# One piece each for the state and the output products of an S5 quarter, at high priority

## The chip, the cores and the metric

The kernel runs on one core of a Trainium2 chip. The metric is the device time of one execution in microseconds (us), as the median of several runs. One execution is also profiled; its trace has start and length of every instruction on TensorE (PE; PEld is its weight load), VectorE (DVE), ScalarE (ACT), GpSimd (POOL) and SyncE (SP), and of the DMA issues.

## The reference, cut to what matters

A decoder trunk of two layers over 256 positions of width 2048. Layer 0 joins dilated softmax attention and gated linear attention. Layer 1, in which the change lies, joins S5 state-space groups with HGRN2 gated linear recurrence:

```
def cd_layer(h, ...):
    z = h @ w_in
    u, qd, fd, idd, gate = jnp.split(z, CD_SPLIT, axis=-1)
    yc = s5_mixer(u, ...)
    f = lower_bound + (1.0 - lower_bound) * jax.nn.sigmoid(fd)
    od = chunked_gated_linear_attention(silu(qd), 1.0 - f, idd, jnp.log(f))
    yd = head_rmsnorm(od, hgrn_norm_g)
    y = jnp.concatenate([yc, yd], axis=-1) * jax.nn.silu(gate)
    return y @ w_out

def s5_mixer(u, ...):      # 64 groups of 16 channels, 64 complex states each
    bu = einsum(bb, u)                     # state products
    x = associative_scan(a * x + bu)       # complex, over positions
    y = c_re x_re - c_im x_im + d_skip * u # output products
    y = gelu(y)
    return y * sigmoid(y @ w_glu + b_glu)
```

## The kernel before

**Weights.** Almost all time is matrix products with streamed weights. `gemm_fm` (L181) and `gemm_tm` (L200) take a weight block in groups of four K-tiles of 128. `load_split` loads a group (`raw`, on SP, three buffers) and cuts it into two *pieces* of two K-tiles. For each piece ScalarE rounds `raw` to `wh` (L168) and VectorE makes the rest `wl = raw - wh` (L169), both urgent and with three buffers. A piece is 24 products of 128x256 in `gemm_fm` or 12 of 128x512 in `gemm_tm`; the first third of them need no `wl`. So ScalarE and VectorE can be at most three pieces ahead, and a `wh` or `wl` can be written only when TensorE has used up the piece three before.

**Hooks.** At the end of each piece `hook()` takes the next *slot* of the list `fillq` and issues what stands in it behind the last product (`issue_after`). The slots hold the S5 work.

**S5.** The 64 groups are done in four quarters, first to fourth, each with eleven slots. In a quarter (`s5_quarter`) `load0` loads the table W (tile `tb`) and the input X; the state products `v_mm` (L583) go to PSUM; VectorE multiplies them with rotation tables (L589 to L592), adds (L601, L602), scans (L603, L604), turns back (L605 to L608), writes X for the outputs (L611) and the sum t2 (L612). The output products `y_mm` are L622 (from X) and L627 (from t2). `finish` copies them to `ys` (ScalarE, L635), writes them to DRAM `s5y` in eight small DMAs (L638; POOL and ScalarE's queue, which also runs ScalarE's work), reads them back in another layout as `yc` (L641, POOL) and forms the GELU: `gw` on ScalarE (L643, L644, L646, L647), L645 and L649 on VectorE. Tables and `yc` have one buffer each. PSUM tiles for all this (`pm`) are four.

**HGRN2.** Beside it, in program order between the weight products, run the two halves of the gated linear attention (`gla`): evacuation of q and k (L359), activations on ScalarE (L666 to L672), `gQ` (L279) and `gT` (L327), then levels h = 1, 2, 4, ..., each with small products on TensorE (L287, L308, L316), a predicated copy (L296) and two multiplications that the next level needs (L324, L325), then L339.

**Order.** The kernel is written in one order; a scheduler that simulates the engines sets the order of each engine's queue by priority and by what it takes to be ready. On the chip each engine works strictly in that order. `urgent()` lifts the priority to the highest. Work without it goes by its place in the program.

## Time and profile before

| | |
|---|---|
| median of 3 runs | 894.18 us (888.37, 894.18, 894.41) |
| profiled execution | 894.61 us, of which the span of the trace 892.7 us |
| granted TensorE clock, mean | 0.996 |
| busy share of the span | PE 98%, DVE 71%, ACT 53%, POOL 6% |
| S5 quarters' products | from 509.9 us to 660.5 us of the span |

The busy share of TensorE is time in which a product runs, small ones too. A row of the timeline has start, length, engine, line, tiles and count, and in brackets the idle time before it with what ended it. The trace counts each product on f32 data of the S5 part as two passes (32 passes for 16 instructions); the rounded weight products take one.

### The profile page before, as it was taken

The numbers are of one execution on the slowest core, as the hardware profiler recorded it, in microseconds if no ns is written. First come the engines' busy times: TensorE is split into PE (matmuls) and PEld (weight loads), VectorE is DVE, ScalarE is ACT, GpSimd is POOL, SyncE is SP. The second block draws the span as 40 slices with busy tenths as digits, with TensorE's granted clock in tenths as the row PEclk, the third lists the DMA queues.
The fourth block names the chain that finished last, engine by engine and source line by source line (L and its number), as shares of the span: only waits on it lengthen the run. The fifth ranks groups of instructions, "written<-read, shape, count | busy, mean of one in ns | idle before, by whom it ended". The sixth has DMA issues, their size and how long they took to land.

```text
span 892.7 us, 18688 instructions
## 1 busy us (share of the span) xinstructions
PE 874.1 (98%) x7728; PEld 804.5 (90%) x7728; DVE 636.0 (71%) x1197; ACT 473.1 (53%) x715; POOL 54.4 (6%) x106
## 2 busy tenths in 40 slices
PE   8999999999999999999999999999999999999995
PEld 8987899888998899999999999899867899988894
DVE  7987975888869868755575586877977655665562
ACT  7654546665655765644443345455545475444451
POOL 0001100111101101000000001100110000000000
PEclk9999999999999999999999999999999999999998
DMA  9827744777756655555575766754654455544432
GB/s 316 318 99 217 257 159 146 231 253 217 264 193 220 223 179 182 206 189 189 190 270 195 267 211 227 247 192 166 222 170 160 183 189 189 189 171 179 176 136 94
DMA packets 40388, 180.40 MB, mean 202 GB/s; under 512 B 12720, under 2 KB 14256, under 8 KB 22768
## 3 DMA queue, kind: packets, MB, share of 16 engines
q1 hardware_dynamic: 29440, 154.99, 49.5%
q0 software_dynamic: 7984, 22.69, 7.7%
q10 hardware_dynamic: 2880, 1.54, 0.6%
q8 instruction: 60, 0.98, 0.4%
q14 instruction: 24, 0.20, 0.1%
HBM read 166.48 MB, written 12.71 MB: 201 GB/s over the span
## 4 chain that ended last, share of the span: by engine, by line
PE 74%; DVE 8%; ACT 6%; DMA 5%; issue 5%; SPq 0%; POOL 0%; POOLq 0%; DVEq 0%; ACTq 0%
PE pg L181 48%; PE pg L200 17%; DVE wl L169 2%; PE pg L758 2%; DMA tabs<-pc 2%; ACT wh L168 1%; PE pm L287 1%; DMA E<-ed 1%; PE pm L339 1%; DMA s5y<-ys 1%; ACT bb L1021 1%; DMA raw<-in_w_dram 1%; ACT x L1039 1%; PE pm L308 1%; DVE PP L1005 1%
## 5 line engine op out<-in xcount | busy, mean ns | idle before, releaser
L168 ACT ACTIVATE wh<-raw 128x1024 fp32r<-128x1024 f32 (+2 forms) x276 | 287.6, 1046 | 325.0 <-PE pg L181 187.6
L169 DVE TENSOR_TENSOR wl<-raw,wh 128x1024 fp32r<-128x1024 f32 (+2 forms) x276 | 332.6, 1207 | 173.7 <-ACT wh L168 165.0
L181 PE MATMUL pg<-xh,wh 128*128 128x256 f32 x1024 | 162.8, 281 | 1.8 <-ACT wh L168 1.7
L181 PE MATMUL pg<-xl,wh 128*128 128x256 f32 x1024 | 163.8, 280 | 0.0
L181 PE MATMUL pg<-xh,wl 128*128 128x256 f32 x1024 | 163.4, 281 | 0.1
L181 PEld LDWEIGHTS pg<-xh,wh 128*128 128x128 f32 x1024 | 137.4, 188 | 3.7 <-ACT wh L168 3.1
L181 PEld LDWEIGHTS pg<-xl,wh 128*128 128x128 f32 x1024 | 138.0, 188 | 0.8 <-issue 0.3
L181 PEld LDWEIGHTS pg<-xh,wl 128*128 128x128 f32 x1024 | 137.9, 189 | 0.8 <-DVE wl L169 0.3
L200 PE MATMUL pg<-wh,xh 128*128 128x512 f32 x320 | 100.4, 395 | 1.8 <-ACT wh L168 1.8
L200 PE MATMUL pg<-wl,xh 128*128 128x512 f32 x320 | 101.0, 396 | 0.5 <-DVE wl L169 0.4
L200 PE MATMUL pg<-wh,xl 128*128 128x512 f32 x320 | 101.0, 395 | 0.0
L200 PEld LDWEIGHTS pg<-wh,xh 128*128 128x128 f32 x320 | 59.3, 188 | 14.8 <-ACT wh L168 2.2
L200 PEld LDWEIGHTS pg<-wl,xh 128*128 128x128 f32 x320 | 59.5, 188 | 14.1 <-DVE wl L169 1.3
L200 PEld LDWEIGHTS pg<-wh,xl 128*128 128x128 f32 x320 | 59.9, 188 | 12.8
L181 PE MATMUL pg<-yh,wh 128*128 128x256 f32 x320 | 50.8, 281 | 0.0
L181 PE MATMUL pg<-yl,wh 128*128 128x256 f32 x320 | 50.6, 281 | 0.0
L181 PE MATMUL pg<-yh,wl 128*128 128x256 f32 x320 | 50.6, 281 | 0.0
L181 PEld LDWEIGHTS pg<-yl,wh 128*128 128x128 f32 x320 | 43.4, 190 | 0.1
L181 PEld LDWEIGHTS pg<-yh,wh 128*128 128x128 f32 x320 | 43.2, 189 | 0.1
L181 PEld LDWEIGHTS pg<-yh,wl 128*128 128x128 f32 x320 | 43.1, 189 | 0.0
L967 POOL DMA_DIRECT2D tabs<-pc x44 | 23.8, 546 | 167.0 <-DVE x L977 43.7
L200 PE MATMUL pg<-wh,yh 128*128 128x512 f32 x96 | 30.1, 394 | 0.0
(350 smaller groups left out, 994.0 us busy)
## 6 DMA issues: line engine op xcount, KB each, us to landing
raw<-in_w_dram SPq DMA_DIRECT2D x100, 1024.0 KB, 5.0
raw<-in_wo_dram SPq DMA_DIRECT2D x28, 1024.0 KB, 4.8
tb<-tabs POOLq DMA_DIRECT2D x8, 768.0 KB, 6.4
tabs<-pc POOLq DMA_DIRECT2D x20, 256.0 KB, 5.7
raw<-in_wg_dram SPq DMA_DIRECT2D x4, 1024.0 KB, 4.8
raw<-in_wo1l_dram SPq DMA_DIRECT2D x4, 1024.0 KB, 4.8
raw<-in_w_dram SPq DMA_DIRECT2D x6, 512.0 KB, 7.4
tabs<-pc POOLq DMA_DIRECT2D x24, 128.0 KB, 4.9
```

The source lines that it names most:

```text
L168: state["wh"] = A.activation(w, r, AF.Copy)
L169: V.tensor_sub(l, r, w)
L181: state["mm"] = T.matmul(ps[:, c], w[:, cs], a[:, kt], start=(i == 0 and n == 0 and c % 2 == 0), stop=(i == last and n == 2), skip_group_c ...
L200: state["mm"] = T.matmul(ps[:, t], a[:, kt, ts_], w, start=(i == 0 and n == 0), stop=(i == last and n == 2), skip_group_check=True)
L287: T.matmul(ps[32 * b:32 * b + 32, t, hd], k[:, hd, r], Q[:, hd, r], start=True, stop=True)
L308: T.matmul(ps[j0:j0 + h, hd, j0 + h:j0 + 2 * h], k[:, hd, b:b + h], Qp[:, hd, b + h:b + 2 * h], start=True, stop=True)
L339: T.matmul(ps[:, (hd - h0) * dv:(hd - h0 + 1) * dv], AT[:, hd, t + j], v[:, j, hd * dv:(hd + 1) * dv], start=(j == 0), stop=(j == t))
L758: T.matmul(ps[:, t, 0:256], a_[:, kt, ts_], w_, start=(kt == 0 and n == 0), stop=(kt == KT - 1 and n == 2), skip_group_check=True)
L967: nc.gpsimd.dma_start(tabs[qt, dst, n], t[src].rearrange("p a b -> p (a b)"))
L1005: V.scalar_tensor_tensor(PP[half[1 - g], g].rearrange("p a b c -> p (a b c)"), x1[half[g]], -1.0, x2[half[g]], op0=OP.mult, op1=OP.subtract)
L1021: A.activation(bb[half[g ^ n], g], z[n][half[g]].unsqueeze(2).to_broadcast([64, 8, 4, 16]), AF.Copy)
L1039: A.activation(v8(x1)[:, r_], cst[:, C_ID64:C_ID64 + 64], AF.Copy, scale=vec[:, V_D + 8 * qt + r_:V_D + 8 * qt + r_ + 1])
```

## The change

Before, a quarter's state products stood in two slots (each in two calls), the second with half of the products' evacuation, and its output products in two more. Now `v_mm` holds all 32 state products in one call, under `urgent()`, with two PSUM tiles at once, and the eight multiplications behind them; it stands in the first slot together with the scan. `y_mm` holds all output products, first all of L622 and then all of L627 (L620 and L625 after), under `urgent()`, in the slot of what was the second half.

```
-        def v_mm(h, n):
-            def go():
-                if n == 0:
-                    t["pv"] = pm_tile()...
-                for w in range(2):
-                    for pr in range(2 * n, 2 * n + 2):
-                        ...T.matmul(pv[...], t["W"][w][us, 4 * h + pr], X[us, g, 4 * h + pr], ...)
-                if n == 1:
-                    V.tensor_mul(t1[:, hs], pv[:, 0], Rc[:, hs])
...
+        def v_mm():
+            X = t["X"]
+            pvs = [pm_tile().rearrange("p (w r c) -> p w r c", w=2, r=4) for _ in range(2)]
+            with urgent():
+                for h, pv in enumerate(pvs):
+                    for w in range(2):
+                        for pr in range(4):
+                            for g in range(2):
+                                us = slice(64 - g * 64, 128 - g * 64)
+                                T.matmul(pv[g * 64:g * 64 + 64, w, pr], t["W"][w][us, 4 * h + pr],
+                                         X[us, g, 4 * h + pr], start=True, stop=True)
+            for h, pv in enumerate(pvs):
+                V.tensor_mul(t1[:, hs], pv[:, 0], Rc[:, hs])
...
-        def y_mm(n):
...
-                for pr in range(4 * n, 4 * n + 4):
+        def y_mm():
+            t["py"] = py = pm_tile().rearrange("p (r c) -> p r c", r=8)
+            with urgent():
+                for pr in range(8):
...
-        return load0, [[load1, v_mm(0, 0), v_mm(0, 1)], [v_mm(1, 0), v_mm(1, 1), scan], [], [], None, [], [], []] + [[y_mm(0)], [y_mm(1)], []]
+        return load0, [[load1, v_mm, scan], [], [], [], None, [], [], [], [], [y_mm], []]
```

Lines behind the first function move up by one, those behind the second by four; the order before the first quarter's state products is unchanged on every engine. Three places of the new order follow.

**Second quarter, VectorE.** From the wl ahead of the state products on, before (`t_...` are t1 to t4, `gw`, `gk`, `gQ`, `gT` as above):

```order
L359 TENSOR_TENSOR gk<-pg,r1b 128x512 x2
L169 TENSOR_TENSOR wl<-raw,wh 128x1024
L589 TENSOR_TENSOR t_6439<-pm,tb_6435 128x256
L590 TENSOR_TENSOR t_6442<-pm,tb_6435 128x256
L591 TENSOR_TENSOR t_6440<-pm,tb_6435 128x256
L592 TENSOR_TENSOR t_6441<-pm,tb_6435 128x256
L601 TENSOR_TENSOR t_6439<-t_6439,t_6440 128x512
L602 TENSOR_TENSOR t_6441<-t_6441,t_6442 128x512
L603 SCALAR_TENSOR_TENSOR t_6440<-tb_6435,t_6439 128x512
L279 TENSOR_TENSOR gQ<-gq,gf 128x1024
L327 TENSOR_TENSOR gT_6811<-gf 128x512
L604 SCALAR_TENSOR_TENSOR t_6442<-tb_6435,t_6441 128x512
```

and after, from the scans on (all eight multiplications stand right ahead of L600):

```order
L602 SCALAR_TENSOR_TENSOR t_6440<-tb_6435,t_6439 128x512
L359 TENSOR_TENSOR gk<-pg,r1b 128x512 x2
L603 SCALAR_TENSOR_TENSOR t_6442<-tb_6435,t_6441 128x512
L169 TENSOR_TENSOR wl<-raw,wh 128x1024
L604 TENSOR_TENSOR t_6439<-t_6440,tb_6435 128x512
L605 TENSOR_TENSOR t_6441<-t_6442,tb_6435 128x512
L169 TENSOR_TENSOR wl<-raw,wh 128x1024
L606 TENSOR_TENSOR t_6440<-t_6440,tb_6435 128x512
L607 TENSOR_TENSOR t_6442<-t_6442,tb_6435 128x512
L610 TENSOR_TENSOR X<-t_6439,t_6441 64x8x63 x2
L279 TENSOR_TENSOR gQ<-gq,gf 128x1024
L327 TENSOR_TENSOR gT_6811<-gf 128x512
```

Then come `L641 gw`, `L611` and two wl. Before, a wl stood between the two halves of the multiplications and the next one behind L604; now none stands from the multiplications to the second scan, and after two more wl a row of seven others follows.

**Second quarter's outputs, ScalarE**, before:

```order
L635 ACTIVATE ys<-pm 128x512
L638 DMA s5y<-ys 16x8x64 x4
L168 ACTIVATE wh<-raw 128x1024 x3
L643 ACTIVATE gw<-yc 128x512
L644 ACTIVATE gw<-gw 128x512
```

after:

```order
L631 ACTIVATE ys<-pm 128x512
L634 DMA s5y<-ys 16x8x64 x4
L168 ACTIVATE wh<-raw 128x1024
L639 ACTIVATE gw<-yc 128x512
L640 ACTIVATE gw<-gw 128x512
```

The first `gw`, which needs yc, moved ahead of two wh. On VectorE the multiplication of `gw` (L645, now L641) moved ahead of the level that makes the inputs of the fourth L287 on gQ. After:

```order
L324 TENSOR_TENSOR gQ<-gQ,gT_6811 128x256x2
L325 TENSOR_TENSOR gk<-gk,gT_6811 128x256x2
L641 TENSOR_TENSOR gw<-gw,yc 128x512
L169 TENSOR_TENSOR wl<-raw,wh 128x1024
L645 SCALAR_TENSOR_TENSOR oT<-gw,yc 128x4x64 x2
L296 COPY_PREDICATED gD<-msk,pm 128x256
L324 TENSOR_TENSOR gQ<-gQ,gT_6849 128x128x4
L325 TENSOR_TENSOR gk<-gk,gT_6849 128x128x4
```

Before, the second L325 stood ahead of L645, right behind two wl and L296; what moved is the dependence of that level on yc.

**Third quarter's outputs and fourth quarter's state products, TensorE**, before (`tb_7139` is the third quarter's table, `tb_7314` the fourth's):

```order
L622 MATMUL pm<-X,tb_7139 64x64
L583 MATMUL pm<-X,tb_7314 64x64 x2
L622 MATMUL pm<-X,tb_7139 64x64 x7
L627 MATMUL pm<-t_7142,tb_7139 64x63 x8
L622 MATMUL pm<-X,tb_7139 64x64 x8
L627 MATMUL pm<-t_7142,tb_7139 64x63 x8
L583 MATMUL pm<-X,tb_7314 64x64 x30
```

after:

```order
L620 MATMUL pm<-X,tb_7139 64x64
L583 MATMUL pm<-X,tb_7314 64x64 x3
L620 MATMUL pm<-X,tb_7139 64x64 x15
L625 MATMUL pm<-t_7142,tb_7139 64x63 x16
L583 MATMUL pm<-X,tb_7314 64x64 x29
```

Ahead of this group, back to the third quarter's state products, stand 80 weight products of 128x256 after, and 103 of them with 15 of 128x512 before.

## The prediction

> **What bounds the kernel now.** I read the page first (busy shares, chain), then the stretch in which the S5 quarters run, then TensorE's waits there.

> ```profile
> span 892.7 us, 18688 instructions
> PE 874.1 (98%) x7728; PEld 804.5 (90%) x7728; DVE 636.0 (71%) x1197; ACT 473.1 (53%) x715; POOL 54.4 (6%) x106
> PE 74%; DVE 8%; ACT 6%; DMA 5%; issue 5%; SPq 0%; POOL 0%; POOLq 0%; DVEq 0%; ACTq 0%
> 500.00:700.00 200.00, 197.74 (x2442) 176.61 (x2441) 153.83 (x232) 98.85 (x143) 17.63 (x34) 1.00 0.59 205
> 880.00:892.00 12.00, 2.42 (x21) 2.21 (x19) 2.44 (x6) 1.07 (x3) 0.55 (x1) 0.70 0.38 149
> ```

> TensorE is busy 98% of the span and carries 74% of the chain. In the 200 us that the change touches it stands still 2.26 us (200 − 197.74), so there is little to win beside its own work, and much to lose. All of the 2.26 us are these three waits (last column: idle time, and what ended it):

> ```profile
> 561.91 0.62 PE L200 MATMUL pg<-wh,xl 128*128 128x512 f32 x2
> 562.75 0.73 PE L200 MATMUL pg<-wl,xh 128*128 128x512 f32 x2 [0.22 <-DVE wl L169]
> ...
> 649.55 0.73 PE L200 MATMUL pg<-wl,xh 128*128 128x512 f32 x2 [0.22 <-DVE wl L169]
> ...
> 653.88 0.63 ACT L643 ACTIVATE gw<-yc 128x512 f32<-128x512 f32 x1 [6.11 <-DMA yc<-s5y]
> ...
> 656.17 0.74 PE L200 MATMUL pg<-wh,xh 128*128 128x512 f32 x2 [1.77 <-ACT wh L168]
> ```

> The first two wait for VectorE's wl, the third for ScalarE's wh, which stood behind a `gw` that waited 6.11 us for `yc` to come back from DRAM. A wait costs more than its idle time: from 561.91 the next start is 0.84 us away instead of 0.46, and the one after it comes 0.1 late, as behind an excursion (510.94 to 511.51 below): 0.48 us, 0.26 more than the idle time. The three cost 0.48 + 0.48 + 2.03 = 3.0 us.

> **What the change saves on TensorE.** Each excursion from the weight products into small ones has a price at its edges:

> ```profile
> 509.31 0.62 PE L181 MATMUL pg<-xh,wl 128*128 128x256 f32 x4
> 509.86 1.15 PE L583 MATMUL pm<-X,tb 64*64 64x64 f32 x32
> 510.94 0.74 PE L181 MATMUL pg<-xh,wh 128*128 128x256 f32 x4
> 511.51 0.62 PE L181 MATMUL pg<-xl,wh 128*128 128x256 f32 x4
> ...
> 533.21 0.62 PE L181 MATMUL pg<-xl,wh 128*128 128x256 f32 x4
> 533.66 0.62 PE L181 MATMUL pg<-xh,wl 128*128 128x256 f32 x4
> 534.21 0.69 PE L622 MATMUL pm<-X,tb 128*64 128x64 f32 x16
> 534.82 0.68 PE L627 MATMUL pm<-t,tb 64*64 64x63 f32 x16
> 535.43 0.74 PE L181 MATMUL pg<-xh,wh 128*128 128x256 f32 x4
> 536.00 0.62 PE L181 MATMUL pg<-xl,wh 128*128 128x256 f32 x4
> ...
> 618.69 2.08 PE L583 MATMUL pm<-X,tb 64*64 64x64 f32 x64
> 620.70 0.62 PE L181 MATMUL pg<-xl,wh 128*128 128x256 f32 x3
> ```

> Four weight products take 0.453 us (533.21 to 533.66), so a piece of 24 takes 2.72 us. The half state excursion costs 511.51 − 509.31 − 2×0.453 = 1.29 us, of which the 32 passes are 1.0 (618.69 to 620.70: 64 in 2.01) and 0.28 is edge. The half output excursion costs 536.00 − 533.66 − 0.907 = 1.43, edge 0.43. One piece for two saves an edge: 0.28 + 0.43 in each of the first two quarters. In the third and fourth the state products already stand together, as the order shows; one edge or two inside the output products go, about 0.4 together; the split of L339 around the third quarter's products gives 0.1 back. Sum: **−1.8 us**, within −1.2 (the first two quarters alone, less that split) and −2.3.

> **What it moves.** VectorE's eight products (L589 to L592) and the scan now stand in one row, without the two weight rests between them that were there before. TensorE must wait wherever a wl comes after it has used up the pieces made ahead. I add up the second quarter by start-to-start distances:

> ```profile
> 545.25 1.15 PE L583 MATMUL pm<-X,tb 64*64 64x64 f32 x32
> ...
> 515.76 0.42 DVE L589 TENSOR_TENSOR t<-pm,tb 128x256 f32<-128x256 f32 x1
> 517.09 0.68 DVE L601 TENSOR_TENSOR t<-t,t 128x512 f32<-128x512 f32 x1
> 518.29 1.22 DVE L603 TENSOR_TENSOR_SCAN t<-tb,t 128x512 f32<-128x512 f32 x1
> 520.54 1.20 DVE L169 TENSOR_TENSOR wl<-raw,wh 128x1024 fp32r<-128x1024 f32 x1
> 521.65 0.69 DVE L605 TENSOR_TENSOR t<-t,tb 128x512 f32<-128x512 f32 x1
> 525.20 1.36 DVE L611 TENSOR_TENSOR X<-t,t 64x504 f32<-64x504 f32 x2
> 526.59 1.29 DVE L359 TENSOR_TENSOR gq<-pg,r1b 128x512 f32<-128x512 f32 x2
> 527.80 1.22 DVE L169 TENSOR_TENSOR wl<-raw,wh 128x1024 fp32r<-128x1024 f32 x1
> ...
> 547.13 0.42 DVE L589 TENSOR_TENSOR t<-pm,tb 128x256 f32<-128x256 f32 x1
> ...
> 555.37 1.20 DVE L279 TENSOR_TENSOR gQ<-gq,gf 128x1024 f32<-128x1024 f32 x1
> 557.09 1.22 DVE L604 TENSOR_TENSOR_SCAN t<-tb,t 128x512 f32<-128x512 f32 x1
> ```

> VectorE starts 1.88 us after TensorE's first state product (547.13 − 545.25). Then: eight products 2.66 (twice 515.76 to 517.09), two sums 1.20, two scans 2.25, evacuation of gk 1.21, wl 1.13, two products 1.2, wl 1.13, two products 1.2, X 1.39, gQ and gT 1.72, gw and L612 1.2, wl 1.22 to its end. With the 1.88 that is 19.4 us. In front of its wl TensorE has 2.2 us of state products, five pieces (13.7) and the third of the sixth that needs no rest (0.9): 16.8 us. It **waits 2.6 us** there. In the first quarter the same sum leaves each wl at least 1.3 us early: nothing.

> The fourth quarter's chain, the same way (nine short steps of the norm at 0.2 us and two more wl in it), ends 2.0 us late. Between: the third quarter's output products now stand 80 weight products behind its state products (9.1 us) instead of 103 and 15 longer ones. X is ready 12.5 us after the first state product and the products of L612 14.4 us after; TensorE is there after 12.2 and 13.4. **Wait 1.3 us.** Bounds of these VectorE terms together (2.6 + 2.0 + 1.3 = 5.9): 0.2 late for each of the first two as the rows show now, and 9 if each chain is 10% slower.

> **A wait that changes place.** `gw` reads yc back from DRAM, and ScalarE and VectorE stand in order behind it:

> ```profile
> 539.71 0.60 ACT L635 ACTIVATE ys<-pm 128x512 f32<-128x512 f32 x1 [0.63 <-PE pm L627]
> ...
> 555.06 0.63 ACT L643 ACTIVATE gw<-yc 128x512 f32<-128x512 f32 x1 [0.24 <-DMA yc<-s5y]
> ...
> 577.24 0.59 ACT L635 ACTIVATE ys<-pm 128x512 f32<-128x512 f32 x1
> 588.98 0.63 ACT L643 ACTIVATE gw<-yc 128x512 f32<-128x512 f32 x1 [1.93 <-DMA yc<-s5y]
> ...
> 587.00 0.76 PE L287 MATMUL pm<-gQ,gk 128*32 128x32 f32 x64
> 591.87 0.33 PE L287 MATMUL pm<-gQ,gk 128*32 128x32 f32 x15
> ```

> In the second quarter yc came 11.15 us after ys was done (577.83 to 588.98), in the first 14.75. Before, three wh stood between; now one does, and on VectorE L645 stands ahead of the level (L296, L324, L325) that the fourth L287 on gQ needs. From the end of the output products TensorE reaches that L287 after 14.6 us: two first blocks 1.4, 100 weight products 11.3, two L287 at 0.9 (591.87 − 587.00 less 35 products). VectorE is done after 0.7 (ys) + 11.15 + gw twice 1.25 + wh 1.0 + wl 1.15 + L649 0.95 + L296 0.35 + L324, L325 1.2 = 17.75. **Wait 3.2 us**; 0 if yc returns in 8 us, 6.8 after 14.75. On POOL the first quarter's yc now stands behind the load of tb, which waits for the second quarter's state products; it is issued near 548 instead of 551, and gf, behind gw on ScalarE, has 2 us to spare: nothing. In the third quarter four wh instead of two stand between ys and gw, so the 1.77 us go. On SP one load of X passes one load of weights that is needed six pieces later: nothing.

> **Sum.** New waits 2.6 + 3.2 + 1.3 + 2.0 = 9.1, plus 0.15 for each of five restarts (0.48 against the 0.33 by which wl was late at 562.75) = 9.9; old waits −3.0; excursions −1.8: **+5.1 us**. The profiled execution took 894.61 (span 892.7 and 1.9 around it), so 899.7; it lies 0.4 above the median shown, 894.18, so I forecast **899.3**.

> **Rivals.**
> - *VectorE keeps up* (0.15). The order is what the scheduler thought would fit. It decides at 16.8 us for a chain that I add up to 19.4; operations would have to be 13% shorter than the rows. Without the three VectorE terms and their restarts (5.9 + 0.6): 892.8, not slower than before. For it: only three small waits exist now. Against it: VectorE works without a gap from 547 on, in rows I have used one by one.
> - *yc returns early* (0.10). With eight us instead of 11.15 the wait at L287 falls away: 896. Against it: 11.15 and 14.75 in the rows.
> - *yc returns late* (0.18). Beyond 11.15 each us is a us of wait; as late as in the first quarter, 3.6 more: 902.9, and 906 where another copy is late too.
> - *The clock falls in the long wait* (0.05). The last row of the first block shows 0.70 where TensorE stands most of 12 us; through 1.77 us of wait the clock stayed at 1.00. Half a clock for the piece after the L287 costs another 2.7: 902. [...]
> - *The pieces aren't in one piece.* The order shows them whole in the first two quarters and cut by a few products in the others; that is in the −1.8 already.

> **How the numbers follow.** Forecast 0.52 (896.5 to 902), the others as given. The range **891.5 to 906** takes in all but the tails; one of three runs before was at 888.37, which no view explains. A measurement here tells about 1% from nothing: slower by over 1% (above 903.1) needs most of the late yc, 0.18; faster by over 1% (below 885.2) has no mechanism, 0.03; the same 0.79.

> **What would show it.** TensorE idle of about 9 us instead of 2.26 between 500 and 700, as waits for wl near 561 and again some 18 us behind the fourth quarter's state products, one at L287 behind a gw that waits for yc for some 7 us, one at the third quarter's L627; excursions of 64 passes at 2.2 to 2.5 us. If the idle time stays near 2 us, the sums on VectorE are wrong; if yc is back in 8 us, the third term is.

## The result and the profile after

| | before | after |
|---|---|---|
| median of 8 runs each, us | 888.25 (886.31 to 894.41) | 899.25 (896.07 to 902.11) |
| profiled execution, us (span) | 894.61 (892.7) | 902.11 (900.3) |
| mean granted clock of the profiled execution | 0.996 | 0.984 |

The change makes the kernel slower: ratio 1.0113, 95% interval 1.0091 to 1.0136. The forecast, 899.3, meets the median after, but not by its own sum: that had +5.1 us from a kernel at 894.2, and the eight runs show +11.0 from 888.25. Two errors of some 6 us met, which is luck.

From the page of the changed kernel, the shares of the chain:

```profile
PE 81%; DVE 7%; DMA 4%; ACT 3%; issue 3%; SPq 0%; POOL 0%; POOLq 0%; DVEq 0%; ACTq 0%
```

The chain shows little: TensorE has 81% of it, more than before. The windows do, for its stretch from 500 to 700 us (stretch, length, busy us of PE, PEld, DVE, ACT and POOL, granted clock, DMA share, GB/s):

```profile
500.00:700.00 200.00, 186.14 (x2288) 167.62 (x2288) 144.67 (x220) 89.51 (x129) 16.88 (x33) 0.96 0.54 186
```

From its timeline, all waits of TensorE over 0.15 us in that stretch:

```profile
552.70 0.73 PE L200 MATMUL pg<-wl,xh 128*128 128x512 f32 x2 [3.21 <-DVE wl L169]
561.73 1.22 PE L200 MATMUL pg<-wl,xh 128*128 128x512 f32 x2 [3.25 <-DVE wl L169]
592.64 1.23 PE L181 MATMUL pg<-xh,wh 128*128 128x256 f32 x4 [2.87 <-ACT wh L168]
596.46 1.08 PE L287 MATMUL pm<-gQ,gk 128*32 128x32 f32 x64 [2.58 <-DVE gk L325]
659.75 0.74 PE L200 MATMUL pg<-wl,xh 128*128 128x512 f32 x2 [1.95 <-DVE wl L169]
```

TensorE stands still 13.86 us in these 200 instead of 2.26, and the clock, 1.00 in the same row of before, is 0.96. The old three waits are gone; five others stand in their place.

**The first two waits.** ScalarE and VectorE between the first quarter's output products and the second quarter's state products, which start at 538.07 (rows of ACTq are DMA issues):

```profile
532.53 0.60 ACT L631 ACTIVATE ys<-pm 128x512 f32<-128x512 f32 x1 [1.56 <-PE pm L625]
533.16 1.65 ACTq L634 DMA_DIRECT2D s5y<-ys  x2
535.01 1.06 ACT L168 ACTIVATE wh<-raw 128x1024 fp32r<-128x1024 f32 x1 [1.87 <-PE pg L181]
536.14 5.67 ACTq L634 DMA_DIRECT2D s5y<-ys  x2
541.92 2.01 ACT L168 ACTIVATE wh<-raw 128x1024 fp32r<-128x1024 f32 x2 [5.85 <-DMA s5y<-ys]
...
538.07 2.08 PE L583 MATMUL pm<-X,tb 64*64 64x64 f32 x64
...
543.01 1.23 DVE L169 TENSOR_TENSOR wl<-raw,wh 128x1024 fp32r<-128x1024 f32 x1 [5.68 <-ACT wh L168]
544.15 0.42 DVE L589 TENSOR_TENSOR t<-pm,tb 128x256 f32<-128x256 f32 x1
```

The second pair of ScalarE's four DMA issues holds its queue for 5.67 us; the wh behind them waits, VectorE's wl waits for that wh, and the eight multiplications stand behind that wl. They start 6.08 us after the first state product (544.15 − 538.07), not 1.88. The list of the engine's instructions names what the issues wait for: completion counters of earlier DMAs. In the traces of before and after SP's loads and ScalarE's issues count on eight of them, here DMAHW0 to DMAHW7. Before:

```
L638 DMA s5y<-ys_6357 16x8x64 [waits Activation_49]
L638 DMA s5y<-ys_6357 16x8x64
L638 DMA s5y<-ys_6357 16x8x64 [waits DMAHW7_49]
L168 ACTIVATE wh<-raw_6534 128x1024 [waits DMAHW6_49,DVE_49,PE_49]
L638 DMA s5y<-ys_6357 16x8x64 [waits DMAHW1_49]
```

and after, where one more waits and two stand behind the wh:

```
L634 DMA s5y<-ys_6357 16x8x64 [waits Activation_49]
L634 DMA s5y<-ys_6357 16x8x64 [waits DMAHW7_49]
L168 ACTIVATE wh<-raw_6534 128x1024 [waits DMAHW6_49,DVE_49,PE_49]
L634 DMA s5y<-ys_6357 16x8x64 [waits DMAHW1_49]
L634 DMA s5y<-ys_6357 16x8x64 [waits DMAHW3_49]
```

Ahead of that last issue DMAHW3 was taken by one of SP's loads of the second quarter's X (before, it was ScalarE's own first issue that took it). In the trace the ten DMAs of SP and ScalarE from SP's load at 532.38 to ScalarE's last issue count in turn on 2, 3, 4, 5, 6, 7, 0, 1, 2 and 3, and ScalarE's last three start 0.02 us after the landing of the DMA that had their counter before: 534.50 (534.48), 536.14 (536.12) and 541.50 (541.48). ScalarE's rows stand in the order of the list: 533.16, 534.50, the wh at 535.01, 536.14, 541.50. The load and the last issue:

```profile
532.81 0.42 SPq L567 DMA_DIRECT2D X<-s5u  x1
...
541.50 0.31 ACTq L634 DMA_DIRECT2D s5y<-ys  x1
```

The load lands 8.7 us after its issue, at 541.5, and the issue starts then. In e2 below the same load is issued at 537.65, and ScalarE's last issue ends at 545.86 (539.47 + 6.39); if it takes the same 0.31 us, it starts at 545.55, 7.9 us after the load.

**The next two.** ScalarE and VectorE behind the second quarter's outputs:

```profile
575.70 0.60 ACT L631 ACTIVATE ys<-pm 128x512 f32<-128x512 f32 x1 [0.42 <-PE pm L625]
576.33 4.49 ACTq L634 DMA_DIRECT2D s5y<-ys  x4
...
590.36 0.63 ACT L639 ACTIVATE gw<-yc 128x512 f32<-128x512 f32 x1 [8.37 <-DMA yc<-s5y]
...
591.68 0.69 DVE L641 TENSOR_TENSOR gw<-gw,yc 128x512 f32<-128x512 f32 x1 [6.89 <-ACT gw L640]
```

yc is back 14.06 us after ys (590.36 − 576.30): its read-back is issued 8.6 us after ys (584.92) and takes 5.4 to land; before, 7.6 (585.39) and 3.6. Why either is longer was not separated. TensorE waits first for the wh behind gw, then for the level behind it on VectorE.

**The clock.** The clock records of the changed kernel's trace last 3.413 us or a whole multiple of it (10.240, 27.307, 549.546), but for the last, which ends with the trace. A row of the windows for each slice of that length, cut where the clock records of that execution change; first the changed kernel around its waits, then the kernel before around its 1.77 us:

```profile
557.96:561.38 3.42, 0.52 (x3) 0.09 (x1) 3.42 (x5) 1.49 (x3) 0.00 (x0) 1.00 0.94 376
561.38:564.79 3.41, 3.06 (x7) 2.48 (x8) 3.41 (x6) 0.10 (x1) 0.00 (x0) 0.50 0.28 48
588.68:592.10 3.42, 1.10 (x10) 0.90 (x8) 0.42 (x1) 1.71 (x3) 0.00 (x0) 1.00 0.02 4
592.10:595.51 3.41, 1.23 (x4) 0.93 (x4) 3.16 (x6) 3.41 (x5) 0.00 (x0) 0.50 0.00 0
595.51:598.92 3.41, 2.46 (x71) 2.43 (x72) 3.41 (x6) 0.01 (x1) 0.00 (x0) 0.50 0.27 36
598.92:602.34 3.42, 3.42 (x18) 3.42 (x18) 1.19 (x3) 1.05 (x1) 0.00 (x0) 0.50 0.67 273
656.95:660.36 3.41, 1.46 (x7) 0.89 (x6) 3.41 (x5) 1.86 (x3) 0.00 (x0) 1.00 0.41 171
660.36:663.77 3.41, 3.41 (x10) 2.65 (x9) 3.19 (x6) 1.53 (x3) 0.00 (x0) 0.50 0.53 159
```

```profile
652.68:656.09 3.41, 1.72 (x8) 1.09 (x6) 2.25 (x4) 2.18 (x4) 0.00 (x0) 1.00 0.87 305
656.09:659.50 3.41, 3.33 (x45) 2.39 (x47) 3.35 (x5) 2.96 (x5) 0.00 (x0) 1.00 0.14 53
```

In these rows a slice with 1.46 us of products or less was followed by one at half clock; behind the one with 1.72 it stayed at 1.00. Once halved, a slice with 2.46 us did not bring it back; behind the one with 3.06 the clock records have full clock. In the halved slices two weight products took 0.85 us instead of 0.46:

```profile
562.75 1.05 PE L200 MATMUL pg<-wh,xh 128*128 128x512 f32 x2
563.60 1.05 PE L200 MATMUL pg<-wh,xl 128*128 128x512 f32 x2
```

Five slices are halved, with 13.6 us of products in them (3.06 + 1.23 + 2.46 + 3.42 + 3.41); 46% of that is lost, 6.3 us.

**The balance** of the two profiled executions, from the first quarter's state products (509.86 before, 503.55 after) to the end of the span: 396.75 against 382.84, so 13.9 us more. Idle time gives 11.6 (13.86 − 2.26), the clock 6.3, the shorter excursions −1.8 as forecast: 16.1. The 2.2 over are not settled; e3 gives a reason for a part of them. The profiled execution is the slowest of the eight; the others had clocks of 0.988 to 0.992, and a halved slice is 0.002 of a mean clock and 1.6 us. By that the fastest (896.07, 0.992) and the slowest (902.11, 0.984) differ by about four slices, 6.4 us, and they lie 6.0 apart; but one run of 901.2 had 0.992 too.

### The profile page after: what moved, and what is told of

It is laid out like the page before. It is cut to its first block, busy times and chain, and to the rows that moved or that the text cites. A ratio compares the mean times of both kernels' runs of the same rounds, so it can differ in the third digit from the quotient of the medians.

```text
span 900.3 us, 18681 instructions
## 1 busy us (share of the span) xinstructions
PE 871.9 (97%) x7728; PEld 803.9 (89%) x7728; DVE 636.7 (71%) x1197; ACT 471.5 (52%) x715; POOL 54.4 (6%) x106
## 4 chain that ended last, share of the span: by engine, by line
PE 81%; DVE 7%; DMA 4%; ACT 3%; issue 3%; SPq 0%; POOL 0%; POOLq 0%; DVEq 0%; ACTq 0%
PE pg L181 47%; PE pg L200 24%; PE pg L754 2%; DVE wl L169 2%; DMA X<-s5u 1%; PE pm L339 1%; ACT wh L168 1%; DMA raw<-in_w_dram 1%; PE pm L287 1%; DMA tabs<-pc 1%; PE pm L583 1%; PE pm L308 1%; DMA yc<-s5y 1%; PE pm L1023 1%; ACT bb L1017 0%
## 5 line engine op out<-in xcount | busy, mean ns | idle before, releaser
L168 ACT ACTIVATE wh<-raw 128x1024 fp32r<-128x1024 f32 (+2 forms) x276 | 287.6, 1046 | 327.4 <-PE pg L181 178.0
L169 DVE TENSOR_TENSOR wl<-raw,wh 128x1024 fp32r<-128x1024 f32 (+2 forms) x276 | 332.4, 1207 | 175.3 <-ACT wh L168 168.9
L181 PE MATMUL pg<-xh,wh 128*128 128x256 f32 x1024 | 164.2, 282 | 4.4 <-ACT wh L168 4.4
L181 PE MATMUL pg<-xl,wh 128*128 128x256 f32 x1024 | 163.3, 280 | 0.0
L181 PE MATMUL pg<-xh,wl 128*128 128x256 f32 x1024 | 163.0, 280 | 0.0
L181 PEld LDWEIGHTS pg<-xh,wh 128*128 128x128 f32 x1024 | 138.5, 190 | 6.1 <-ACT wh L168 5.4
L181 PEld LDWEIGHTS pg<-xl,wh 128*128 128x128 f32 x1024 | 138.4, 190 | 0.7 <-issue 0.3
L181 PEld LDWEIGHTS pg<-xh,wl 128*128 128x128 f32 x1024 | 138.1, 190 | 0.4
L200 PE MATMUL pg<-wl,xh 128*128 128x512 f32 x320 | 101.7, 399 | 8.4 <-DVE wl L169 8.4
L200 PE MATMUL pg<-wh,xh 128*128 128x512 f32 x320 | 101.8, 398 | 0.0
L200 PE MATMUL pg<-wh,xl 128*128 128x512 f32 x320 | 101.2, 397 | 0.0
L200 PEld LDWEIGHTS pg<-wl,xh 128*128 128x128 f32 x320 | 60.0, 190 | 22.7 <-DVE wl L169 9.7
L200 PEld LDWEIGHTS pg<-wh,xl 128*128 128x128 f32 x320 | 60.7, 190 | 13.0
L200 PEld LDWEIGHTS pg<-wh,xh 128*128 128x128 f32 x320 | 60.0, 190 | 13.0
L181 PE MATMUL pg<-yh,wh 128*128 128x256 f32 x320 | 50.1, 277 | 0.0
L181 PE MATMUL pg<-yh,wl 128*128 128x256 f32 x320 | 49.5, 277 | 0.0
L181 PE MATMUL pg<-yl,wh 128*128 128x256 f32 x320 | 49.5, 277 | 0.0
L181 PEld LDWEIGHTS pg<-yh,wh 128*128 128x128 f32 x320 | 42.6, 188 | 0.0
L181 PEld LDWEIGHTS pg<-yh,wl 128*128 128x128 f32 x320 | 42.4, 188 | 0.0
L181 PEld LDWEIGHTS pg<-yl,wh 128*128 128x128 f32 x320 | 42.4, 188 | 0.0
L200 PE MATMUL pg<-wh,yh 128*128 128x512 f32 x96 | 30.1, 395 | 0.0
```

What stands on the lines that cost most here:

```text
L168: state["wh"] = A.activation(w, r, AF.Copy)
L169: V.tensor_sub(l, r, w)
L181: state["mm"] = T.matmul(ps[:, c], w[:, cs], a[:, kt], start=(i == 0 and n == 0 and c % 2 == 0), stop=(i == last and n == 2), skip_group_c ...
L200: state["mm"] = T.matmul(ps[:, t], a[:, kt, ts_], w, start=(i == 0 and n == 0), stop=(i == last and n == 2), skip_group_check=True)
```

## The experiments

Each kernel was timed beside the kernel before; the ratios are to that.

### e1: the state products alone in one piece

```
-        def y_mm():                      # one piece, urgent
+        def y_mm(n):                     # two halves, as before
-        return load0, [[load1, v_mm, scan], [], [], [], None, [], [], [], [], [y_mm], []]
+        return load0, [[load1, v_mm, scan], [], [], [], None, [], [], [], [y_mm(0)], [y_mm(1)], []]
```

> Only the state products of a quarter stand in one piece at high priority; the output products stand in two slots as in the kernel before. My theory (two causes: ScalarE's queue is blocked by its own issues of s5y after the first quarter's outputs, so wh and wl come late; and gw stands two wh earlier behind yc) gives this kernel neither of the two, since here ScalarE issues s5y as before (three, a wh, one) and gw stands behind three wh again. What is left is the row of VectorE work without a wl: a wait of about 2.6 us near 560 and about 2 us behind the fourth quarter's state products, with half a clock after each (about 1.5 us each), less the old waits (3.0) and two edges (0.6): about 4 us over before, 892 (890 to 894.5). Rival (the row of VectorE work alone makes the first two waits of the changed kernel, whatever ScalarE does): they stay at 6.5 us together, 896 to 897. Rival (the one piece at high priority costs time on TensorE itself): excursions of 64 passes longer than 2.3 us.

Measured: 891.26 us, ratio 1.0023 (0.9997 to 1.0049). Its two waits of TensorE over 0.15 us:

```profile
558.57 0.72 PE L200 MATMUL pg<-wl,xh 128*128 128x512 f32 x2 [2.48 <-DVE wl L169]
649.68 0.74 PE L200 MATMUL pg<-wl,xh 128*128 128x512 f32 x2 [2.90 <-DVE wl L169]
```

And the windows for the slices around the second:

```profile
644.69:648.10 3.41, 2.10 (x10) 1.38 (x8) 3.40 (x6) 3.38 (x5) 0.00 (x0) 1.00 0.89 293
648.10:651.51 3.41, 1.83 (x8) 1.43 (x8) 3.38 (x5) 0.74 (x2) 0.00 (x0) 1.00 0.03 12
651.51:654.92 3.41, 3.41 (x29) 2.54 (x27) 3.41 (x7) 2.08 (x3) 0.00 (x0) 1.00 0.87 308
```

Without the blocked ScalarE queue and the early gw, VectorE's row without a wl costs 2.48 us, close to the 2.6 of the prediction. 2.90 us of wait left the clock alone, because the border of two slices fell into it and either still had 1.83 us of products or more; 1.95 us in the changed kernel, all in one slice, halved it.

### e2: the output products alone in one piece

```
-        def v_mm():                      # one piece, urgent
+        def v_mm(h, n):                  # four calls, as before
-        return load0, [[load1, v_mm, scan], [], [], [], None, [], [], [], [], [y_mm], []]
+        return load0, [[load1, v_mm(0, 0), v_mm(0, 1)], [v_mm(1, 0), v_mm(1, 1), scan], [], [], None, [], [], [], [], [y_mm], []]
```

> Only the output products stand in one piece at high priority; the state products stand in two slots as before. My theory: after the first quarter's outputs ScalarE issues two DMAs, a wh and two more, and the last ones wait some 5 us as in the changed kernel; wh and wl come 4 us late, and since VectorE's row behind the second quarter's state products had nothing to spare before (0.22 us of wait), this shows as one or two waits for wl of about 4 us together between 545 and 565, with some half clock behind (1.5); gw stands behind three wh, so no wait at L287. With 1.2 us saved at the edges: about 4 us over before, 892.5 (890 to 894.5). Rival (the state products in one piece make all of the loss): about 1 us faster than before, 887, and no wait over 0.5 us near 550.

Measured: 893.29 us, ratio 1.0050 (1.0019 to 1.0080). ScalarE's second pair of issues, and the wait that follows on TensorE:

```profile
539.47 6.39 ACTq L635 DMA_DIRECT2D s5y<-ys  x2
545.96 2.01 ACT L168 ACTIVATE wh<-raw 128x1024 fp32r<-128x1024 f32 x2 [5.43 <-DMA s5y<-ys]
...
560.22 0.73 PE L200 MATMUL pg<-wl,xh 128*128 128x512 f32 x2 [3.15 <-DVE wl L169]
```

So the block on ScalarE comes with the output products, and it costs 3.15 us and a halved slice with no state products moved at all. The rival, which had it at 887, falls. The profiled execution (895.08) is not to be read as a whole: its first state product starts at 507.65, some 4 us later than in the changed kernel (503.55), as that of before does. From there to the end it takes 385.6 us, the kernel before 382.9.

### e3: the second quarter's gw back behind three wh

```
+            with tc.issue_after(state["wh"].ins):     # in a slot of the next quarter
                 A.activation(gw, yc, AF.Square)
```

> The changed kernel with one thing put back: the second quarter's first gw stands behind the wh behind which it stood before (three wh behind ys instead of one), on VectorE L641 goes behind the level again; all else in the order stays. My theory: the two waits of 2.87 and 2.58 us near 592 and 596 go, and with them the 10 us of half clock that start there (3 to 4 us of time): about 9 us less than the changed kernel, 890 (888 to 892.5). The waits near 552 and 561 (6.5 us) and near 660 (2 us) stay. Rival (yc is late anyway, and whatever stands behind gw waits for it, so the wait moves to a later wh): 896 to 899, with a wait of 2 us or more for wh between 595 and 605. Rival (half clock costs nothing beside the idle time): 893.5.

Measured: 892.82 us, ratio 1.0040 (1.0012 to 1.0069): 6.4 less than the changed kernel by the medians, not 9. No wait is left between 565 and 610. The two waits ahead of it:

```profile
552.78 1.22 PE L200 MATMUL pg<-wl,xh 128*128 128x512 f32 x2 [3.76 <-DVE wl L169]
561.81 0.74 PE L200 MATMUL pg<-wl,xh 128*128 128x512 f32 x2 [0.58 <-DVE wl L169]
```

And the windows for the two slices behind the start of the first:

```profile
551.72:555.14 3.42, 2.36 (x6) 1.88 (x7) 3.42 (x5) 3.42 (x7) 0.00 (x0) 0.50 0.00 0
555.14:558.55 3.41, 3.41 (x10) 2.64 (x9) 3.37 (x5) 2.28 (x3) 0.57 (x1) 0.50 0.66 233
```

The wait did not move to another wh. Of the two waits for wl the second shrank here, since two slices behind the first were halved and TensorE, at half clock, came to the second wl that much later. By this reading half clock ahead of a wait is paid once, not twice; e9 fits it, with one halved slice between the two and a second wait of 1.66.

### e4: no DMA of s5y on ScalarE's queue

```
-                    (nc.gpsimd if s % 2 else nc.scalar).dma_start(
+                    nc.gpsimd.dma_start(
```

> The changed kernel with all eight DMAs of s5y on POOL's queue, none on ScalarE's; since yc is then expected later, the second quarter's gw also stands behind three wh, as in e3. My theory: after the first quarter's outputs wh follows at once, VectorE's eight products start about 1.9 us after the second quarter's first state product instead of 6.1, and of the 6.5 us of wait near 552 and 561 some 2.6 stay (the row without wl); the waits near 592 and 596 go as in e3; 2 us near 660 stay: 3 to 4 us less than e3, 887 (884.5 to 890). Rival (VectorE's row alone makes the first waits): they stay, and the time is that of e3. Rival (eight issues in a row on POOL bring yc back so late that gw holds up ScalarE elsewhere): a wait for wh of over 2 us behind the second or third quarter's outputs, and slower than e3.

Measured: 890.82 us, ratio 1.0014 (0.9989 to 1.0038). The second quarter's state products on TensorE, VectorE's first multiplication behind them, and all waits of TensorE over 0.2 us:

```profile
538.29 2.08 PE L583 MATMUL pm<-X,tb 64*64 64x64 f32 x64
...
540.18 0.42 DVE L589 TENSOR_TENSOR t<-pm,tb 128x256 f32<-128x256 f32 x1
...
557.75 1.22 PE L200 MATMUL pg<-wl,xh 128*128 128x512 f32 x2 [2.55 <-DVE wl L169]
647.06 0.73 PE L200 MATMUL pg<-wl,xh 128*128 128x512 f32 x2 [1.95 <-DVE wl L169]
```

The row starts 1.89 us after the first state product, and the prediction's two terms for VectorE, 2.6 and 2.0, stand there as 2.55 and 1.95. The time is over what I expected (887), and only 2.0 under e3, which the intervals don't tell apart. The traces do: in the first two quarters VectorE's order is that of e3, and ScalarE's differs from it by the DMA issues alone. From the second quarter's first state product to its first output product e4 takes 31.1 us (538.29 to 569.40), e3 34.5 and the changed kernel 35.4 (538.07 to 573.43). So the blocked queue is a cause, worth 3.4 us there, with gw in the same place.

### e5: work added into the waits of e3

The edit, shortened:

```
+            # behind the products wh x xl of K-tiles 4 and 8 of v's block
+            for _ in range(6):  ...   # the two products of that K-tile again; 5 for K-tile 8
```

> e3 with work added where TensorE waited: twelve products (wh with xl) said again ahead of the wl that it waited for near 552, ten ahead of the one near 561; 22 products of 0.2285 us, 5.0 us of work. The repeats add to v a second time what is small there, so this kernel's v is not that of the reference. My theory of the clock: the profile's clock records stand on a grid of 3.41 us whose place differs from execution to execution, and a slice of the grid in which TensorE stands for over about 1.8 us is followed by one at half clock. Here no slice near 550 has that much, so e3's 6.8 us at half clock from 551.7 go; since VectorE sets when the wl come, the added 5.0 us cost nothing: from the second quarter's first state product to its first output product as long as in e3 within 1.5 us, and the whole 892 to 894 (behind it the order differs a little: the fourth quarter's row of VectorE as in e1). Rival (half clock has another cause, such as the small products): half clock stays near 552. Rival (the added work is paid): 5 us longer.

Measured: 889.74 us, ratio 0.9990 (0.9966 to 1.0015). The second quarter's state products, the two waits and the output products:

```profile
536.78 2.08 PE L594 MATMUL pm<-X,tb 64*64 64x64 f32 x64
551.95 0.73 PE L210 MATMUL pg<-wl,xh 128*128 128x512 f32 x2 [0.99 <-DVE wl L170]
560.97 0.73 PE L210 MATMUL pg<-wl,xh 128*128 128x512 f32 x2 [0.97 <-DVE wl L170]
571.25 1.15 PE L631 MATMUL pm<-X,tb 128*64 128x64 f32 x32
```

And the window of the slice ahead of the first wait's end, which has 0.76 us of idle time:

```profile
548.30:551.71 3.41, 2.65 (x12) 1.85 (x10) 3.41 (x5) 2.03 (x4) 0.00 (x0) 1.00 0.01 5
```

With 5.0 us more work the stretch from 536.78 to 571.25 is 34.47 us, in e3 34.49 (537.60 to 572.09): the added work is free, VectorE sets the pace. No slice is halved any more, so it was the standing still that halved the clock. It does not price the clock there, since in e3 the halved slices lay ahead of a wait. The whole is even less than I expected; what else differs from e3 is the fourth quarter's order, where its wait is 0.54 us and not 1.93.

### e6: e4 with a wl between the halves of the multiplications

```
-        return load0, [[load1, v_mm, scan], [], [], [], None, ...
+        return load0, [[load1, v_mm], [], [], [], [mul1, scan], ...   # mul1: second half, behind that piece's wl
```

The scan moves to the slot of the second half with it.

> e4 with a wl put back between the two halves of VectorE's eight products in the first and second quarter, as before; TensorE's products stay in one piece at high priority. My theory: the 2.55 us of wait near 557 and the half clock behind it go (at most 0.5 us stays), about 2 to 3 us near the fourth quarter stay: 888 (886 to 890). Rival (X and the sum now stand one or two wl later, so TensorE waits at the second quarter's output products instead): a wait of 1 to 3 us at L620 or L625 near 570, and no gain on e4 (890.8). Rival (the wait is what the one piece costs, wherever wl stands): 2.5 us stay near 557.

Measured: 889.48 us, ratio 0.9996 (0.9970 to 1.0021). The wait near 557 is gone and so is every halved slice between 500 and 700:

```profile
500.00:700.00 200.00, 196.02 (x2443) 175.13 (x2443) 155.26 (x235) 98.86 (x144) 25.21 (x49) 1.00 0.58 201
```

With wl put back, the time is that of the kernel before. But s5y stands on POOL's queue here, and that alone takes the kernel before to 885.97 (e8): beside e8 the changed products, even with wl put back, are 3.5 us slower by the medians, though the intervals of the two ratios still overlap (0.9937 to 0.9982 in e8). Of its 3.98 us of idle time 2.33 stand among the small products of L287 with nothing that ended them (records of products may be missing there), 0.75 at the L287 behind gw and 0.68 at the fourth quarter's wl. The wait at L620 or L625 that a rival had is not there; whether 889.5 is a gain on e4's 890.8 the intervals don't tell.

### e7 and e8: s5y off ScalarE's queue, with the output products in one piece and without

e7 is e2 and e8 the kernel before, each with the edit of e4.

> e2 (output products alone in one piece) with all DMAs of s5y on POOL's queue; gw of the third quarter then stands behind two more wh. My theory: of the waits of e2 the 3.15 us near 560 with the half clock behind go, since ScalarE is no longer blocked, and the 1.82 us near 657 go with the later gw; 1.2 us of edges are saved: 887 or a little less, 885 to 888.5, which would beat both kernels by a little. Rival (the eight issues on POOL bring yc so late that gw holds ScalarE up): a wait for wh of over 1.5 us, and 889 or more.

> The kernel before with all DMAs of s5y on POOL's queue and nothing else changed by hand; gw of the third quarter stands behind two more wh, and that of the fourth later too. My theory: the 1.77 us near 656 go, nothing else changes: 886.5, 885 to 888 (against 888.3). It is the yardstick for e7: what e7 has over it is the price or gain of the output products in one piece alone, about 1 us. Rival (ScalarE's issues cost nothing in the kernel before and POOL's queue is the slower one): 888.3 or more.

Measured: e7 886.28 us, ratio 0.9955 (0.9931 to 0.9978); e8 885.97, ratio 0.9959 (0.9937 to 0.9982). The same stretch of e7, then of e8:

```profile
500.00:700.00 200.00, 198.00 (x2453) 176.91 (x2452) 155.56 (x237) 99.95 (x144) 25.22 (x49) 1.00 0.58 202
```

```profile
500.00:700.00 200.00, 199.28 (x2449) 176.97 (x2449) 155.18 (x237) 99.41 (x144) 25.22 (x49) 1.00 0.57 202
```

Both are about 0.4% faster than the kernel before. The gain doesn't come from the output products in one piece, since e8 has it without them: e7 saves its edges but waits 1.50 us at the L287 behind gw, e8 0.64, and the 1.2 us that I gave e7 over e8 don't show. The edit of e8 is the queue alone, but the scheduler's order follows it (gw later, several wl in other places on VectorE), and which of these gives the gain was not separated. In the 200 us e8 stands still 0.72 us instead of 2.26, which is 1.5 of the some 3.6 us gained; the rest is not found.

Beside e4, e7 prices the state products: both have the output products in one piece and s5y on POOL, and e4 has the state products in one piece too. It is 4.5 us slower, and the intervals of the ratios (0.9989 to 1.0038 and 0.9931 to 0.9978) lie apart. So with ScalarE's queue clear, the output products in one piece cost nothing, and the state products in one piece still do.

### e9: the change without the high priority

```
-            with urgent():      # around the state products and around the output products
```

> The changed kernel without the high priority of the two pieces. In the first two quarters this leaves every engine's order as it is; in the third and fourth the pieces move by one weight piece. My theory (ScalarE's queue blocked after the first quarter's outputs, gw early in the second, the clock after each wait) has nothing to do with the priority: the waits near 552, 561, 592 and 596 stay, about 6.5 and 5.5 us, and the time is that of the changed kernel, 899 (896 to 902). Rival (the priority drives the small products ahead of what VectorE and ScalarE have ready, and makes the waits): 893 or less, and less than 3 us of wait between 545 and 600.

Measured: 901.6 us, ratio 1.0134 (1.0100 to 1.0169), that of the changed kernel. All four waits of the first two quarters stay, 3.88, 1.66, 2.34 and 3.08 us; the first:

```profile
553.07 1.22 PE L200 MATMUL pg<-wl,xh 128*128 128x512 f32 x2 [3.88 <-DVE wl L169]
```

In the first two quarters the priority is not what costs; the slots are. The fourth quarter's wait, 1.95 us with the priority, is not there: behind 600 the only wait up to 700 is 0.44 us at 691.63. The time is no shorter for it.

## Why the prediction was right, and where it was not

- **Excursions, −1.8: right where it was measured.** The first quarter's state products cost 2.22 us (from 503.01 to 506.14, less two times 0.453) against 2 × 1.29; the output products 2.37 (529.71 to 532.99) against 2 × 1.43. Each saves 0.4 to 0.5 in the quarter; the other quarters were not added up.
- **Old waits, −3.0: right.** None of the three is left.
- **"It waits 2.6 us there": the sum was right, its start wrong.** The step that failed is "VectorE starts 1.88 us after TensorE's first state product". It took 6.08, because I priced what moved on SP and POOL but not ScalarE's own four DMA issues and what they wait for, here a load of X on SP. The term came out as 3.21 + 3.25 = 6.5 us of wait. With the issues on POOL it is 2.55 (e4), in e1 2.48.
- **"Wait 3.2 us" at L287: right in kind, mis-sized.** yc took 14.06 us, not 11.15; the two waits are 5.45 together. The prediction's rival of a late yc had a us of wait for a us of delay, and it came near that (2.25 for 2.9). e3 confirms place and cause: with gw behind three wh, both waits are gone.
- **Third quarter's outputs, 1.3: absent.** VectorE's sum was right: L611 was done 14.3 us after the first state product (624.56 to 638.85), against 14.4. TensorE came later than I had it: to the first L620 after 12.9 us instead of 12.2, and to L625 after 14.6 instead of 13.4, with three of the fourth quarter's state products and the outputs of L620 between (637.43 to 639.13). Behind them TensorE did not work strictly in the order of the list: from 639.89 to 640.06 five passes of L583 start among the last six of L625.
- **VectorE keeps up, as a rival: fell.** e4 waits 2.55 and 1.95 where it would have none.
- **Fourth quarter's chain, 2.0: right,** 1.95 (it is not there without the high priority, e9); the first quarter's chain, nothing: right.
- **The clock: the rival at 0.05 happened,** in three places, behind waits of 3.25, 2.87 and 1.95 us; I had put it at one wait of 3.2. Its half clock is measured: 0.50 in the slices above, and in the kernel before from 884.79 to 892.70, without a product; with 1.00 ahead of it that is the 0.70 of the 12 us. The slices of 3.41 us lie differently in each execution: a border at 656.09 before, at 656.95 in the changed kernel. TensorE need not stand still for the whole of one: 1.95 us sufficed (e5 shows that filling the waits takes the half clock away). Reading "1.77 us of wait stayed at 1.00" as safety was my error: its slice had 1.72 us of products, and behind it the clock stayed at 1.00.
- **The base.** I put +5.1 on one execution of 894.61 and took the three runs' median, 894.18, as typical; eight runs give 888.25. The profiled execution of before had lost some 6 us ahead of the change, where the order is the same. In 90 us of layer 0's out-projection it did 767 products, the changed kernel's 796, both at full clock and without idle time:

```profile
370.00:460.00 90.00, 90.00 (x767) 90.00 (x766) 55.08 (x61) 44.87 (x53) 2.00 (x7) 1.00 0.54 195
...
367.00:457.00 90.00, 90.00 (x796) 90.00 (x796) 57.70 (x66) 46.34 (x55) 2.00 (x7) 1.00 0.59 207
```

The chance for slower by over 1% was 0.18, and the ratio, 1.0113, lies just past that bound. The time was met because a base that was 6 us high and a change that was priced 6 us low cancel.

## What to carry to other kernels

Before moving work on an engine whose queue also issues DMAs, list what each of those issues waits for and when that lands: here two DMA issues that waited for completion counters kept the arithmetic behind them waiting for 5.7 us. An engine that ran without slack (0.22 us of wait in the row before) passed a delay of its supplier on: VectorE started 4.2 us later than summed (6.08 − 1.88), and TensorE's waits were 3.9 us longer than without that delay (6.46 against 2.55 in e4). So a chain is summed from the latest of its inputs, the supplier's queue included. A wait of TensorE had a second price here, by the estimate above up to 1.6 us for each halved slice, which depended on where the slice's border fell. And a time that is met is checked term by term: here the change and its base were each 6 us off.

## What the runs showed of the hardware that was not expected

Why products of the same form took 0.117 us each in one execution and 0.113 in another (767 and 796 in 90 us, both at full granted clock) stays open; no run here was aimed at it, and e2's profile has the slower ones there too. Why the load of X that held ScalarE's issue took 8.7 us to land stays open as well.
